# Attention heads in a written TensorE order, a new stacking of q, and the last v projection in a slot of its own

## The chip, the cores and the metric

The kernel runs on one core of a Trainium2 chip. The metric is the device time of one launch in microseconds, as a median of three runs. TensorE multiplies matrices and transposes, into PSUM; VectorE, ScalarE and GpSimd do the elementwise work; SyncE's queue (and for a few small loads ScalarE's) issues the DMA transfers.

## The reference

One layer of a decoder on 512 positions of 1024 columns: a half-step SwiGLU FFN, a mixer with two groups of 8 attention heads of 64 columns, and a second half-step FFN. Each is normed before and after and modulated by a conditioning vector. The change concerns the mixer alone:

```python
p = n @ w_in[l]
qa, ka, va, qi, ki, wi, qb, kb, vb = jnp.split(p, IN_SPLITS, axis=-1)
ki = rmsnorm(ki, g_kidx[l])
oa = rmsnorm(dsa_sparse_attention(qa, ka, va, qi, ki, wi, rel_bias), g_out_a[l])
ob = rmsnorm(stick_breaking_attention(qb, kb, vb), g_out_b[l])
o = jnp.concatenate([oa, ob], axis=-1) @ w_out[l]
```

Group A is sparse: an indexer of 8 heads scores each key, `sum_h w_h * relu(q_h . k)`, the 128 best keys of each query stay, and softmax runs over them with a bias by distance. Group B is stick-breaking attention: the weight of key s is `sigmoid(z_s)` times the product of `1 - sigmoid(z_j)` over the keys j between s and the query.

## The kernel before

Every fp32 matrix product is made of three products of rounded parts (high by high, high by low, low by high). `w_load` brings 128x1024 weights over SyncE's queue into one of three buffers `raw`, rounds them (ScalarE, line 132) and subtracts for the low part (VectorE or GpSimd, line 138); `raw` comes free with the subtraction.

A tile framework traces the program and orders each engine's instructions by its own estimate of when they are ready; each engine then runs its list strictly in that order. A block `manual_schedule` keeps the written order for the engines it names. Here it is used for other stages (ScalarE and VectorE in `down`), not in the mixer. Tiles of one tag share a number of buffers, and a new tile waits until an old one is read.

The mixer (`mixer`, lines 605 to 640) runs so:

- `indexer` (from line 678): `proj_block` projects the index keys and three of the four pairs of index queries into four PSUM banks, first half of the positions, then the second. When a bank is done its end step runs. `end_ki` transposes the keys (line 702), norms them with eight scalings (line 716) and transposes them back doubled (line 719). `end_q` splits a pair of query heads and stacks them by `stack`. Then 8 heads x 3 row blocks of scores (lines 739 to 742) are summed up, head by head, with the projection of the first unit between them.
- `topk` (lines 764 to 778): 16 rounds of `max` and `match_replace` for each of three row blocks (256, 384 and 512 columns), on VectorE: 33 steps each. They are traced at the fifth unit, but may run whenever VectorE is free.
- Eight units of two heads, four of group B, then four of group A. `qkv_steps` gives the projections of the next unit as small steps: the load of k's weights, then 4 steps each for k, q and v, of six matmuls each. `fill` runs a step between the parts of the present unit. In `unit` both heads' score tiles (`attn_b`, lines 896 to 906; `attn_a`, 915 to 923) and transposes (`transposed`, line 888) come first, then for each head the product with v (line 863), three fills, a copy and the output transposes (line 871). The last unit's fills are steps of the output projection (`out_steps`).
- `stack` (line 780) puts the high and the low part of a head on top of each other in one tile by three transfers of 64 partitions. The third writes what the first reads, so it waits for it:

```python
a = self.kq_tile(1)[0]
for dst, src in ((a[0:64], x[0:64]), (a[64:128], y[0:64]), (x[0:64], y[64:128])):
    self.nc.sync.dma_start(out=dst.bitcast(F32), in_=src.bitcast(F32))
```

k is stacked twice (high with high, low with low), q once. Tiles of tag `kq` share 13 buffers.
- At the fifth unit stand the bias rows and windows of group A (`bias_windows`: two matmuls, a store, eight loads on ScalarE's queue) and the norm of group B's output (`o_norm`, lines 564 to 585).
- After the mixer, `mixer_out` norms group A's output and `down` finishes the output projection.

## Time and profile before

| | |
|---|---|
| runs | 1100.77, 1100.91, 1100.93 us; median 1100.91 |
| profiled execution | 1099.78 us; span of its instructions 1098.0 us |
| TensorE matmuls | 1056.6 us busy (96%), x5111 |
| TensorE weight loads | 869.1 us (79%) |
| VectorE / ScalarE / GpSimd | 583.5 (53%) / 405.6 (37%) / 146.0 us (13%) |
| granted clock of TensorE, mean | 0.994 |

Busy shares are averages over stages. The first FFN runs to about 390 us, the norm before the mixer to 420, the indexer to 469, the stick-breaking units to 581, the sparse units to 690, the output projection to 727, and the rest is the second FFN, in which TensorE has nearly no idle time. A matmul's end is modelled in a profile: consecutive matmuls overlap in it. "issue" is time in which an engine waited for nothing that the profile shows. Times in rows are from the start of the span.

### The profile page before, as it was taken

Reading aid. Unit: us, or ns where it says so; the run is one execution under the profiler, and the core shown is the slowest. Engines: PE = TensorE matmul, PEld = TensorE weight load, DVE = VectorE, ACT = ScalarE, POOL = GpSimd, SP = SyncE. Lnnn points to the kernel's source line nnn. Section 1 sums busy time; section 2 is a strip of 40 time slices with the busy share of each in tenths; the row PEclk is TensorE's granted clock in tenths of the full one; section 3 lists DMA queues with packets and bytes.
Section 4 is the critical chain, followed back from the end, with each engine's and each line's share of the span. In section 5 each row is a group of like instructions: output and inputs, shape, how many; then the busy total and the mean of one; then the engine's idle time right before and its main releaser. Section 6 shows DMA issues by size and latency. Waiting matters only on the chain.

```text
span 1098.0 us, 13367 instructions
## 1 busy us (share of the span) xinstructions
PE 1056.6 (96%) x5111; PEld 869.1 (79%) x5111; DVE 583.5 (53%) x988; ACT 405.6 (37%) x711; POOL 146.0 (13%) x103
## 2 busy tenths in 40 slices
PE   3899999999999998999999999999999999999997
PEld 2778888888888888877777878789888888888886
DVE  5979888834223174499995444582333333322313
ACT  3342222222212363455556656472232222221221
POOL 2000000000000522423332413320000000000030
PEclk9899999999999999999999999999999999999999
DMA  9969887732222503533334433303333333222222
GB/s 282 294 210 325 297 283 266 248 96 95 91 89 92 164 20 93 144 96 96 92 97 142 132 101 110 116 21 114 96 96 96 96 96 96 96 96 96 96 77 77
DMA packets 171364, 146.06 MB, mean 133 GB/s; under 512 B 7132, under 2 KB 142460, under 8 KB 171300
## 3 DMA queue, kind: packets, MB, share of 16 engines
q1 hardware_dynamic: 169792, 142.97, 42.4%
q10 hardware_dynamic: 1508, 2.24, 0.6%
q8 instruction: 40, 0.66, 0.2%
q14 instruction: 24, 0.20, 0.1%
HBM read 132.04 MB, written 2.13 MB: 122 GB/s over the span
## 4 chain that ended last, share of the span: by engine, by line
PE 82%; DVE 8%; issue 3%; DMA 3%; POOL 2%; ACT 1%; SPq 1%; DVEq 0%; POOLq 0%; ACTq 0%
PE mm L276 15%; PE mm L277 15%; PE mm L278 15%; PE mm L319 8%; PE mm L320 8%; PE mm L318 8%; PE mm L298 3%; PE mm L468 2%; DVE at L904 1%; DMA ra<-in_w_ada_dram 1%; PE at L793 1%; PE at L794 1%; PE tp L888 1%; DMA kq<-kq 1%; POOL rstd L143 1%
## 5 line engine op out<-in xcount | busy, mean ns | idle before, releaser
L132 ACT ACTIVATE wh<-raw 128x1024 fp32r<-128x1024 f32 x156 | 164.3, 1058 | 432.0 <-PE mm L277 139.4
L276 PE MATMUL mm<-nl,wh 128*128 128x512 f32 x808 | 321.2, 398 | 0.0
L277 PE MATMUL mm<-nh,wh 128*128 128x512 f32 x808 | 316.3, 392 | 0.0
L278 PE MATMUL mm<-nh,wl 128*128 128x512 f32 x808 | 316.1, 391 | 0.0
L138 DVE TENSOR_TENSOR wl<-raw,wh 128x1024 fp32r<-128x1024 f32 (+1 forms) x120 | 147.0, 1227 | 223.7 <-ACT wh L132 223.5
L278 PEld LDWEIGHTS mm<-nh,wl 128*128 128x128 f32 x808 | 151.8, 188 | 31.4
L276 PEld LDWEIGHTS mm<-nl,wh 128*128 128x128 f32 x808 | 152.3, 188 | 28.8 <-ACT wh L132 0.3
L277 PEld LDWEIGHTS mm<-nh,wh 128*128 128x128 f32 x808 | 152.0, 188 | 29.0
L320 PE MATMUL mm<-wh,hT 128*128 128x512 f32 x352 | 138.9, 394 | 0.0
L319 PE MATMUL mm<-wh,hT 128*128 128x512 f32 x352 | 138.8, 394 | 0.0
L318 PE MATMUL mm<-wl,hT 128*128 128x512 f32 x288 | 113.9, 396 | 0.0
L138 POOL TENSOR_TENSOR wh<-raw,wh 128x1024 fp32r<-128x1024 f32 x10 | 25.2, 2534 | 653.7 <-ACT wh L132 653.6
L521 DVE TENSOR_TENSOR sg<-sg,mm 128x512 f32<-128x512 f32 x44 | 30.1, 685 | 105.1 <-PE mm L278 91.0
L138 POOL TENSOR_TENSOR wl<-raw,wh 128x1024 fp32r<-128x1024 f32 x27 | 64.7, 2397 | 106.3 <-ACT wh L132 98.1
L320 PEld LDWEIGHTS mm<-wh,hT 128*128 128x128 f32 x352 | 66.2, 188 | 15.6
L319 PEld LDWEIGHTS mm<-wh,hT 128*128 128x128 f32 x352 | 66.2, 188 | 15.5
L153 DVE SCALAR_TENSOR_TENSOR acc<-ra,sc,acc 128x1024 f32<-128x1024 f32 x49 | 62.7, 1279 | 4.5 <-DMA ra<-in_w_ada_dram 4.0
L318 PEld LDWEIGHTS mm<-wl,hT 128*128 128x128 f32 x288 | 54.1, 188 | 13.1
L468 PE MATMUL mm<-nh,wh 128*128 128x512 f32 x96 | 33.7, 429 | 7.2 <-ACT nh L447 6.9
L132 ACT ACTIVATE hT<-sg 128x512 fp32r<-128x512 f32 x44 | 27.8, 632 | 27.4 <-DVE sg L521 27.4
L138 DVE TENSOR_TENSOR pt<-tp,pt 128x512 fp32r<-128x512 f32 (+1 forms) x48 | 27.2, 594 | 18.8 <-ACT pt L132 18.7
L793 PE MATMUL at<-kq 128*128 128x256 f32 (+2 forms) x88 | 31.3, 357 | 3.4 <-DMA kq<-kq 3.4
(208 smaller groups left out, 1244.9 us busy)
## 6 DMA issues: line engine op xcount, KB each, us to landing
ra<-in_w_ada_dram SPq DMA_DIRECT2D x56, 512.0 KB, 5.6
raw<-in_w_ffn_gate_dram SPq DMA_DIRECT2D x44, 512.0 KB, 4.2
raw<-in_w_ffn_up_dram SPq DMA_DIRECT2D x44, 512.0 KB, 4.3
raw<-in_w_ffn_down_dram SPq DMA_DIRECT2D x44, 512.0 KB, 3.4
raw<-in_w_in_dram SPq DMA_DIRECT2D x28, 512.0 KB, 3.5
kq<-kq SPq DMA_DIRECT2D x84, 128.0 KB, 2.4
ra<-in_w_ada_dram SPq DMA_DIRECT2D x32, 256.0 KB, 5.5
raw<-in_w_out_dram SPq DMA_DIRECT2D x8, 512.0 KB, 3.8
```

The source lines that it names most:

```text
L132: return self.nc.scalar.activation(hi, src, AF.Copy)
L138: return a, (eng or self.nc.vector).tensor_sub(lo, src, hi.bitcast(F32))
L153: nc.vector.scalar_tensor_tensor(acc, raw, sc[:, k:k + 1], acc, op0=ALU.mult, op1=ALU.add)
L276: nc.tensor.matmul(ps[0:m, c], w[0][:, k, :], n[1][:, k, c], start=k == 0, stop=False)
L277: nc.tensor.matmul(ps[0:m, c], w[0][:, k, :], n[0][:, k, c], start=False, stop=False)
L278: return nc.tensor.matmul(ps[0:m, c], w[1][:, k, :], n[0][:, k, c], start=False, stop=k == KD - 1)
L298: mm = self.nc.tensor.matmul(ps[0:m, c], wt[:, k, :], nt[:, k, c], start=j + k == 0, stop=j == 2 and k == KD - 1)
L318: nc.tensor.matmul(ps, lh[:, t], wl, start=n == 0, stop=False)
L319: nc.tensor.matmul(ps, ll[:, t], wh, start=False, stop=False)
L320: nc.tensor.matmul(ps, lh[:, t], wh, start=False, stop=n == len(ks) - 1)
L468: nc.tensor.matmul(banks[j], ws[j][l][:, k, :], n[r][:, k, :], start=k + o == 0, stop=k == KD - 1 and o == 2)
L793: nc.tensor.matmul(ps, q[hd][:, t], kl[hd][:, 0:n], start=True, stop=False)
```

## The change

- `slot` takes the place of `unit`. One slot holds the four score tiles of a new head, one fill after each, and behind each of the first three fills a group of transposes of the head before; then a fill, that head's product with v, a fill, and its output transposes. Sixteen heads make sixteen slots, and a last slot has no new head. All that TensorE gets there stays in the written order.
- v is copied into a tile of its own at the projection's end, and transposed one fill into the next unit (`turn_v`). The load of the next k's weights goes to the first step of v's projection. The last unit's k and q projections, its v projection and the output projection are spread over the last slots with empty steps between them.
- q is split into two tiles of a new tag, and four transfers build its two stacked tiles.
- In the indexer, `proj_block` takes steps ahead of a bank's second half (`mids`), and the second half of `end_ki` goes there; the eight scalings become a product and a copy; the low parts of two index weights are made by VectorE instead of GpSimd; the scores go by row block, and steps of the first top-k are traced among them.
- The bias rows are computed in the first unit, their inputs loaded before the indexer; the windows are still loaded at the fifth unit. `o_norm` of group B becomes four steps ahead of fills of the fifth unit.

The diff, cut to its core:

```diff
-    def proj_block(self, ws, n, banks, ends=()):
+    def proj_block(self, ws, n, banks, ends=(), mids={}):
...
+                if half == 1 and b in mids:
+                    mids[b]()
...
+            for u in range(len(cols) - 1):
+                steps[u][8] = both(first[u + 1], steps[u][8])
+            for k, f in zip((4, 8), loads):
+                steps[-1][k] = both(f, steps[-1][k])
+            gap = [lambda: None]
+            kq, v = steps[-1][:8], steps[-1][8:]
+            steps[-1] = kq[:2] + gap + kq[2:4] + gap + kq[4:] + gap * 2
+            steps.append(v + gap + [outs[0]] + [last[-1]] + [outs[1]] + gap * 2 + [outs[2], outs[3]] + gap + outs[4:])
+            for u in range(len(cols) - 1):
+                steps[u + 1][1] = both(last[u], steps[u + 1][1])
+            self.steps = [first[0]] + steps[0]
...
-            with tc.issue_after(load.ins):
+            with tc.issue_after(load.ins), tc.manual_schedule(engines={mybir.EngineType.PE}):
+                old = None
+                for u in range(len(cols)):
+                    self.steps = steps[u + 1]
+                    if u == 4:
+                        for f in top:
+                            f()
+                        U = self.bias_windows(scr)
...
+                    for hd in range(2):
+                        if u == 4 and hd == 1:
+                            for k, f in enumerate(self.o_norm(1, self.o, oT, tp, pool, 3)):
+                                self.steps[4 + k // 2] = both(f, self.steps[4 + k // 2])
+                            self.o = None
+                        if u == 0 and hd == 1:
+                            scr = self.bias_rows()
...
+                        self.slot(new, old)
+                        old = new
+                self.slot(None, old)
...
-        ws += [(self.w_cols(w_in, C_QI + j * 128, 128, alloc if j == 2 else None,
-                            nc.gpsimd if j < 2 else None), 128) for j in range(3)]
+        ws += [(self.w_cols(w_in, C_QI + j * 128, 128, alloc if j == 2 else None), 128) for j in range(3)]
...
-            for i in range(NT):
-                for c in range(2):
-                    nc.vector.tensor_scalar(k2[:, i, c, :], kk[:, i, :], r[:, i:i + 1], None, op0=ALU.mult)
+            nc.vector.tensor_mul(k2[:, :, 0, :], kk, r.unsqueeze(2).to_broadcast([128, NT, 64]))
+            nc.vector.tensor_copy(k2[:, :, 1, :], k2[:, :, 0, :])
+            st["k2"] = k2
+
+        def end_ki2():
+            k2 = st["k2"]
...
-        self.proj_block(ws, n, banks, [end_ki] + [lambda ps=ps: end_q(ps) for ps in banks[1:]])
+        self.proj_block(ws, n, banks, [end_ki] + [lambda ps=ps: end_q(ps) for ps in banks[1:]],
+                        {3: end_ki2})
...
-        todo = [f for hd in range(6) for f in scores(hd)]
+        todo = [score(*c) for c in [(1, hd) for hd in range(6)] + [(2, hd) for hd in range(3)]
+                + [(1, 6), (1, 7)] + [(2, hd) for hd in range(3, 8)] + [(3, hd) for hd in range(8)]]
...
+        for k, f in enumerate(todo):
+            f()
+            if k % 3 < 2:
+                self.fill()
+            if k > 6:
+                tops[0].pop(0)()
+        return notsel, tops[0] + [f for fs in zip(*tops[1:]) for f in fs], load
...
-            q = self.kq_tile()
+            q = [pool.tile([128, 512], F32R, tag="tm", name="tm", bufs=2) for _ in range(2)]
...
-            st["q"] = self.stack(q[0], q[1])
+            st["q"] = a, b = self.kq_tile()
+            for dst, src in ((a[0:64], q[0][0:64]), (b[64:128], q[0][64:128]), (a[64:128], q[1][0:64]), (b[0:64], q[1][64:128])):
+                nc.sync.dma_start(out=dst.bitcast(F32), in_=src.bitcast(F32))
...
+        def turn_v():
+            vt = st["vt"]
...
+    def slot(self, new, old):
+
+        for i in range(NT):
+            if new:
+                new["tile"][i]()
+            self.fill()
+            if old and i < 3:
+                self.transposed(old, i)
+        if old:
+            self.fill()
+            self.product(old)
+            self.fill()
+            self.output(old)
+        else:
+            self.fill(2)
```

## Rows read from the trace of the kernel before

**Rows 1.** Engine use by stretch: length; busy us of PE, PEld, DVE, ACT, POOL; clock; DMA.

```profile
436.00:466.00 30.00, 30.00 (x143) 25.05 (x143) 13.00 (x22) 14.28 (x29) 12.04 (x8) 1.00 0.56 148
466.00:581.00 115.00, 110.05 (x588) 86.72 (x587) 111.28 (x258) 62.20 (x137) 38.43 (x21) 1.00 0.36 98
581.00:690.00 109.00, 107.62 (x582) 87.20 (x583) 51.58 (x132) 64.19 (x149) 34.54 (x19) 1.00 0.42 122
```

**Rows 2.** Waits of PE, 466 to 690 us: us in total, times, longest.

```profile
PE at L793 <- DMA kq<-kq: 3.4, 4, 1.2
PE tp L888 <- DVE x L906: 2.3, 5, 0.6
```

**Rows 3.** Timeline of PE: start, length, instruction.

```profile
489.66 1.46 PE L863 MATMUL at<-pt,v 128*128 128x512 f32 x8
490.95 0.45 PE L276 MATMUL mm<-nl,wh 128*128 128x512 f32 x1
...
491.70 0.40 PE L276 MATMUL mm<-nl,wh 128*128 128x512 f32 x1
...
492.39 0.39 PE L276 MATMUL mm<-nl,wh 128*128 128x512 f32 x1
```

**Rows 4.** Timeline of PE in the indexer; idle time before in brackets.

```profile
424.87 0.52 PE L298 MATMUL mm<-nh,wh 128*128 128x256 f32 x3
426.35 0.33 PE L719 MATMUL tp<-ident,k 128*128 128x128 f32 x1 [0.97 <-DVE k L716]
...
428.82 0.33 PE L719 MATMUL tp<-ident,k 128*128 128x128 f32 x1 [1.90 <-DVE k L716]
```

**Rows 5.** Engine use by stretch, in the indexer.

```profile
430.00:432.00 2.00, 2.00 (x12) 2.00 (x11) 1.30 (x3) 1.11 (x2) 0.00 (x0) 0.52 0.83 242
432.00:434.00 2.00, 2.00 (x14) 2.00 (x13) 0.58 (x1) 1.09 (x2) 0.00 (x0) 0.62 0.41 96
```

**Rows 6.** Chain that ended last, near 490 us: start, length, what.

```profile
486.33 1.07 ACT wh L132
487.47 2.42 POOL wl L138
489.91 0.37 SPq L120
490.37 3.88 DMA kq<-kq
```

**Rows 7.** Timeline of DVE in the indexer.

```profile
425.88 3.53 DVE L716 TENSOR_SCALAR k<-kk,rstd 128x64 f32<-128x64 f32 x8 [1.13 <-POOL rstd L143]
```

**Rows 8.** Groups on DVE by shape, 469 to 581 us: busy us, mean ns, idle.

```profile
L904 DVE TENSOR_TENSOR_SCAN at<-at,ones 128x512 f32<-128x512 f32 x8 | 9.8, 1222 | 0.2
...
L772 DVE MAX8 m<-tk 128x8 f32<-128x256 f32 x15 | 6.2, 415 | 0.0
L775 DVE MATCH_REPLACE8 tk<-m,tk 128x256 f32<-128x256 f32 x15 | 6.1, 409 | 0.0
...
L906 DVE TENSOR_TENSOR x<-at,x 128x511 f32<-128x511 f32 x8 | 5.4, 676 | 0.0
```

**Rows 9.** Timeline of DVE ahead of the norm before the mixer.

```profile
387.62 0.21 DVE L339 TENSOR_SCALAR ss<-ss 128x1 f32<-128x1 f32 x1 [13.04 <-ACT f L332]
```

**Rows 10.** Tile view of the top-k: ns min/median/max, first and last start.

```profile
L778 DVE TENSOR_TENSOR ns<-tk,sco x3: 680/1640/2115, 572.7 to 576.3; 128x256 bf16<-128x256 f32 x1, 128x384 bf16<-128x384 f32 x1, 128x512 bf16<-128x512 f32 x1
```

**Rows 11.** Groups on ACT by shape, 466 to 581 us: busy us, mean ns, idle.

```profile
L902 ACT ACTIVATE x<-at 128x512 f32<-128x512 f32 x8 | 4.8, 599 | 7.1 <-PE at L900 7.1
```

**Rows 12.** Tile view of the stacked tiles, 466 to 690 us: ns min/median/max.

```profile
L138 POOL TENSOR_TENSOR kq<-q,kq x7: 1282/1301/1471, 489.8 to 659.2; 128x512 fp32r<-128x512 f32 x7
...
DMA to landing us min/median/max: 2.2/2.7/4.4
```

**Rows 13.** Timeline of PE around a group of two transposes and one matmul.

```profile
474.50 0.40 PE L277 MATMUL mm<-nh,wh 128*128 128x512 f32 x1
...
475.26 0.28 PE L793 MATMUL at<-kq 128*128 128x256 f32 x1
```

More of the change, by code (lines that the diff above doesn't have):

```diff
@@ L585, in o_norm @@
             self.normed = self.split(oT[0][:, :, ts], oT[1][:, :, ts], x, nc.vector if i % 2 else nc.gpsimd)
+        return [lambda i=i: one(i) for i in range(NT)]
     def bank(self, pool):
@@ L595, in mixer_out @@
             oT = [[pool.tile([128, 4, S], F32R, tag=f"oT{c}", name="oT", bufs=1) for c in range(2)], oTb]
-            self.o_norm(0, oa, oT[0], tp, pool)
+            for f in self.o_norm(0, oa, oT[0], tp, pool):
+                f()
             g = self.gate_row(1, pool)
@@ L640, in mixer @@
-        return o, banks
+            first, last, steps, ready = map(list, zip(*[self.qkv_steps(*c) for c in cols]))
+            both = lambda *fs: lambda: [f() for f in fs]
+            loads, outs, banks = self.out_steps(oT)
+            for u in range(len(cols) - 1):
[4 more added lines that the diff above has]
+            kq, v = steps[-1][:8], steps[-1][8:]
@@ L642, in out_steps @@
+        return self.o, banks
     def out_steps(self, oT):
-        banks = [self.bank(p) for p in (self.pj, self.pj, self.pj, self.at)]
-        cks = []
+        banks, cks = [], []
         def load(n):
@@ L650, in mms, with run, bias_rows @@
         def mms(i, c):
-            return lambda: self.down_mms(banks[i], lambda k: [t[:, k - 4, :] for t in oT], OUT_KS, i, cks[c])
-        return [load(0), load(2)] + [mms(i, c) for c in range(2) for i in range(NT)], banks
-    def bias_windows(self):
-        nc, pool, pj, d = self.nc, self.pool, self.pj, self.d
-        hot = pool.tile([32, 640], F32, tag="p", name="hot", bufs=3)
-        rb = pool.tile([32, NH], F32, tag="rb", name="rb")
-        nc.scalar.dma_start(out=hot, in_=d["onehot"])
-        nc.scalar.dma_start(out=rb, in_=d["rel_bias"])
-        fr = pool.tile([NH, 640], F32, tag="p", name="fr", bufs=3)
+            def run():
+                if not banks:
+                    banks.extend(self.bank(p) for p in (self.pj, self.pj, self.pj, self.at))
+                self.down_mms(banks[i], lambda k: [t[:, k - 4, :] for t in oT], OUT_KS, i, cks[c])
+            return run
+        return [load(0), load(2)], [mms(i, c) for c in range(2) for i in range(NT)], banks
+    def bias_rows(self):
+        nc, pool, pj = self.nc, self.pool, self.pj
+        rb, hot = self.table
+        fr = pool.tile([NH, 640], F32, tag="pt", name="fr", bufs=4)
         for c0, c1 in ((0, 512), (512, 640)):
@@ L752, in indexer @@
         end_q(ps)
-        for f in todo + scores(6) + scores(7):
-            f()
-            self.fill()
         notsel, tops = [self.tri_gt], []
@@ L835, in end_v @@
             st["v"] = v
-        steps = [weights(ck)]
+        steps = []
         both = lambda *fs: lambda: [f() for f in fs]
@@ L844, in qkv_steps @@
             steps += mms
-        return steps, st
+        return weights(ck), turn_v, steps, st
     def fill(self, n=1):
@@ new lines, in product @@
+    def product(self, h):
+        nc, pool, at = self.nc, self.pool, self.at
+        v, hd = h["v"]["v"], h["hd"]
+        ps = at.tile([128, 512], F32, tag="at", name="at")
+        c = 0
+        for j in range(NT):
+            w = (NT - j) * 128
+            for p in h["pt"]:
+                nc.tensor.matmul(ps[:, j * 128:512], v[:, j, hd, :], p[:, PT_OFF[j]:PT_OFF[j] + w],
+                                 start=c == 0, stop=c == 7)
+                c += 1
+        h["ot"] = pool.tile([128, 512], F32, tag="w2", name="ot", bufs=3)
+        nc.scalar.activation(h["ot"], ps, AF.Copy)
@@ new lines, in transposed @@
+    def transposed(self, h, g):
+        if g == 0:
+            h["pt"] = [self.pool.tile([128, 1280], F32R, tag="pt", name="pt", bufs=4) for _ in range(2)]
+        c0, c1, js = ((0, 512, (0,)), (512, 1024, (1, 3)), (1024, 1280, (2,)))[g]
+        t = self.tp.tile([128, 512], F32, tag="tp", name="tp")
+        for j in js:
+            for i in range(j, NT):
+                c = PT_OFF[j] - c0 + (i - j) * 128
+                s = P_OFF[i] + j * 128
+                self.nc.tensor.transpose(t[:, c:c + 128], h["p"][:, s:s + 128], self.ident)
+        self.split(h["pt"][0][:, c0:c1], h["pt"][1][:, c0:c1], t[:, 0:c1 - c0])
@@ L923, in attn_a @@
             nc.scalar.activation(pp, pp, AF.Exp, scale=-1.0, bias=nm[:, i:i + 1], accum_out=den[:, i, hd:hd + 1])
-            self.fill((0, 1, 1, 2)[i])
-        return p
+        return p, [lambda i=i: one(i) for i in range(NT)]
 @with_exitstack
```

127 lines of the change are left out of this document (49 added, 78 removed).

## The prediction

> **What bounds the kernel now.** Read first how busy the engines are in the mixer, by stretch [rows 1]. From 436 to 466 us (scores of the indexer) TensorE has no idle time. From 466 to 581 us (the four stick-breaking units) it idles 115.00 - 110.05 = 4.95 us, and in the four sparse units, 581 to 690 us, 1.38 us. So TensorE bounds all three, and only its idle time and its clock can be won. The same rows show a second engine close behind: VectorE is busy 111.28 of 115 us in the stick-breaking stretch, because the top-k steps fill it, and only 13.00 of 30 us in the stretch before.
>
> Next, what TensorE waits for between 466 and 690 us [rows 2]: 3.4 us in 4 waits before the first q*k product of a unit (line 793, for the copies that stack q and k), and 2.3 us in 5 waits before the transposes of a head's weights (line 888, for VectorE's last product). With two smaller ones that is the 6.3 us of idle time of rows 1, in 11 waits. The profile makes each too short: a 512-column matmul is drawn 0.40 us long though three starts in steady flow lie 0.69 us apart, 0.23 each [rows 3], so 0.17 us of a wait lies under a drawn end. 6.3 + 11 x 0.17 = 8.2 us.
>
> Third, the indexer. TensorE idles 0.97 and 1.90 us before two of the four transposes of the normalised index keys (line 719) [rows 4]. Right after, its granted clock is 0.52 and then 0.62 of full speed for 2 us each [rows 5], a mixture of the two levels 1.2 and 2.4 GHz; the 5 us before hold the two pauses.
>
> Last, why q arrives late, in the chain of waits at the unit border near 490 us [rows 6]: GpSimd's subtraction of weights frees a buffer, SyncE's queue then issues the weight load that waited for it, and only behind that the copies of q, which take 3.88 us.
>
> **The change, part by part.**
>
> *Index keys.* Eight scalings of 64 columns, 3.53 us from 425.88 [rows 7], become a product and a copy of 256 columns; a pass of VectorE over 256 columns takes 0.41 [rows 8], so 0.8 us, and the keys are ready near 426.7. Their transposes are now traced behind the third bank. When TensorE paused at 425.4, it had done 3 of that bank's 24 matmuls [rows 4]; the other 21 at half of 0.23 us fill 2.4 us, so it comes to the transposes near 427.8, 1.1 us after the keys. Both waits go: 2.87 + 2 x 0.17 = 3.2 us (0 if the keys were late again). The slow clock follows the pauses; without them 2 x 0.48 + 2 x 0.38 = 1.7 us come back (0 if another pause takes their place).
>
> *Two subtractions of weights* move from GpSimd to VectorE, which has 13.04 us without work just there [rows 9]: 0. Without that cover each would hold up the norm by its length, less than GpSimd's 2.42 [rows 6].
>
> *Scores and top-k.* The scores go by row block instead of by head, so the first top-k (256 columns) can start early, 13 of its 33 steps among the scores: 13 x 0.41 [rows 8] = 5.4 us of VectorE's work move into the stretch with 17 us of idle VectorE [rows 1]. 111.3 - 5.4 = 105.9 us are left in the stick-breaking stretch. If that loses its nine waits (4.95 + 9 x 0.17 = 6.5) it lasts 108.5 us, and VectorE is busy 98% of it, as before. On the time: 0. Today the top-k's last result starts at 576.3 us [rows 10], 4.7 us ahead of the first sparse unit; it has 6.5 us less time and 5.4 us less work ahead of it.
>
> *The pipeline.* A slot holds a new head's four score tiles, the former head's three groups of transposes, six fills of six matmuls (1.4 us each), the product with v (1.29 us [rows 3]) and the output transposes (some 0.45). From a head's fourth tile to its first transposes lie four fills, the product, the output and a tile (0.4): 7.7 us. In it ScalarE makes two passes of 0.60 [rows 11] and VectorE one of 1.22 and one of 0.68 [rows 8]: 3.1 us. So the 2.3 us of waits at line 888 and the smaller ones go, unless VectorE's queue holds 4.6 us of other work in front. The written order also takes away TensorE's way out, to put other matmuls ahead of a late operand. Its weak place is the output: between the product and the output transposes stands one fill, 1.4 us, for a copy of 0.60 on ScalarE; behind a rounding of weights of 1.07 [rows 6] it is 0.3 us late. I take 0.1 for each of 16 heads, 1.6 us (0 to 4.8).
>
> *q by four transfers.* Before, three copies, the third held until the first has read; now four from two new tiles without order among them, one issue more per unit on SyncE's queue. From q's last matmul to the next unit now lie four fills, two tiles, two groups of transposes, the product and the output, some 9.1 us. q needs two passes of ScalarE (1.2), 1.30 on GpSimd [rows 12] behind a subtraction of 2.42, and 2.7 (2.2 to 4.4) to land [rows 12]: 7.6, at worst 9.3. All 3.4 us go, or all but 0.2 at a border. The load of the next k's weights is traced four fills earlier, behind q's copies instead of in front: load, rounding and subtraction are the same ones, and only the following copies stand behind it.
>
> *More groups.* The transposes of v stand alone and come one slot step later; the sparse heads have three groups in place of two: some 2 groups more for each of 8 units. A stretch of one matmul, a group of two and one matmul takes 474.50 to 475.26, 0.76 us [rows 13]; two matmuls take 0.46 and two transposes, at half that pitch, 0.23. So 0.07 a group, with 16 of them 1.1 us lost (0 to 1.1).
>
> *Moved off the border.* The bias rows (two matmuls, two copies, a store and, ahead of them, two loads on ScalarE's queue) go into the first unit, the norm of the stick-breaking output into fills of the fifth: the same work, 0. Eight window loads go on ScalarE's queue, six of them into buffers that the top-k frees. Where the queue stands at one of them, ScalarE stands until the top-k ends: 0 to 3 us, taken as 0 since that end lies ahead of the unit. The last output has no fill behind it, but ready matmuls of the second half of the output projection can stand there: 0 to 0.9 (the copy of 0.60 and a share of what is ahead of it), taken as 0.3.
>
> **Sum:** 3.2 + 1.7 + 8.2 - 1.6 - 1.1 - 0.3 = 10.1 us less. The profiled execution took 1099.78 us (span 1098.0, 1.8 around it) and so would take 1089.7; the median of the runs is 1.1 us above it: 1100.9 - 10.1 = 1090.8. What follows the mixer is TensorE with little waiting, so it moves up as a whole. 0.2% (2.2 us) is what a measurement of this kernel can tell from no change.
>
> **The rivals.**
>
> *A, VectorE keeps the stretch.* For it: 97% busy there [rows 1], a fixed order, and top-k steps between the urgent ones. Then the waits for VectorE stay or move to the product: 2.9 us with 7 x 0.17, 4.1 of the 8.2, are not won: 1100.9 - 6.0 = 1094.9 (1093.5 to 1098.7). Against: 4.6 us of slack for each head. The Trainium skill (Perfetto Trace Analysis, Identifying the Most-Contended Engine) judges TensorE by its weight-load share and works first on the engine with the highest occupancy; in this stretch that is VectorE, 97% against 75%, and by that rule this rival is the likely one. The trace has TensorE wait for VectorE's product only 2.3 us.
>
> *B, no change.* The scores by row block hold the eight q tiles of the indexer until the end: with two key tiles and four of the first unit's k 14, and the pool has 13. The last copy of that k waits for a score of the third block; if v's weight load stands behind it in SyncE's queue, the v projection waits for a landing, a rounding and a subtraction, 3.88 + 1.07 + 2.42 = 7.4 us [rows 6], and the slow clock comes again, 1.7: 1100.9 - 1.0 = 1099.9. Against: the load needs nothing from the copy and can be issued first.
>
> *C, slower.* TensorE stands in every slot, since its order can't step aside, for VectorE's last product of the head. It decides at (10.1 + 2.2) / 16 = 0.77 us a slot; at 1 us the time is 1090.8 + 16 = 1106.8. It needs VectorE to answer 5 us late; now it costs TensorE 0.6 us at the longest [rows 2].
>
> *D, slower by the copies.* If q's four half-height copies went one after another, 4 x 2.7 behind 4.9 of preparation is 15.7 against 9.1: 6.6 us at 7 borders, 46 us, near 1141. The Trainium skill (DMA: Bandwidth & Descriptors, Rules for kernel authors) says that transfers to two disjoint halves of the partitions serialise. The rows speak against it at this size: a copy beside a weight load four times its size lands in 3.88 [rows 6], the median is 2.7 [rows 12].
>
> **How the numbers follow.** Forecast (1087 to 1093.5) 0.53; better, down to 1085, if outputs and groups cost nothing, 0.06; A 0.20; B 0.10; C 0.08; D 0.03. Faster is 0.53 + 0.06 + 0.20 = 0.79, the same 0.10, slower 0.11. The range, 1086 to 1100.2, takes in A and B and leaves out C, D and the tip of the better case, some 0.14.
>
> **What would show it.** Right: no pause at the key transposes and full clock to 440 us; no wait of a first q*k product for kq; the former 115 us at 107 to 110, the sparse stretch at 107 to 109. Wrong: transposes or products that wait in most slots, a top-k that ends after the first sparse tile, or a wait between 445 and 470 us for a copy of k or for v's weights.

## The result, and the profile after

The changed kernel takes 1112.72 us (median of 4 runs, 1111.89 to 1113.2) against 1100.92 us of the kernel before: a ratio of 1.0108, 95% interval [1.0096, 1.012]. It is 11.8 us slower where 10.1 us less was forecast. The profiled execution took 1111.89 us, with a span of 1109.6. All times are of fast executions; one execution of `e6_windows_pool`, of 6007.8 us, is left out.

The same stretches as in [rows 1], with the one behind the indexer's pauses and three short ones, in the view of engine use by stretch (length; busy us of PE, PEld, DVE, ACT, POOL; clock; DMA):

```profile
436.00:466.00 30.00, 28.39 (x134) 23.26 (x133) 23.80 (x60) 15.05 (x31) 12.21 (x7) 1.00 0.49 126
466.00:581.00 115.00, 109.05 (x577) 87.22 (x576) 99.16 (x220) 60.92 (x132) 38.76 (x21) 0.99 0.44 120
581.00:690.00 109.00, 100.03 (x527) 81.06 (x534) 50.44 (x121) 60.55 (x137) 29.38 (x16) 0.97 0.32 88
430.00:434.00 4.00, 4.00 (x24) 3.27 (x23) 3.37 (x3) 1.17 (x3) 2.15 (x1) 1.00 0.95 245
493.00:496.00 3.00, 3.00 (x12) 2.52 (x11) 1.63 (x6) 0.94 (x4) 0.00 (x0) 0.50 0.83 224
602.00:605.00 3.00, 3.00 (x10) 2.52 (x11) 2.49 (x6) 1.86 (x4) 0.57 (x1) 0.50 0.65 180
663.00:666.00 3.00, 2.81 (x9) 2.29 (x10) 0.30 (x2) 0.49 (x2) 0.00 (x0) 0.58 0.58 195
```

The part of the indexer that was to be won is won: 430 to 434 us runs at full clock, where [rows 5] had 0.52 and 0.62. But TensorE now idles 1.61, 5.95 and 8.97 us in the three stretches of [rows 1], where it idled 0, 4.95 and 1.38, and its clock is about half in three new places (0.50, 0.50 and 0.58). The waits of PE from 466 to 700 us say what ended the idle time (us in total, times, longest):

```profile
PE tp L931 <- ACT ot L921: 6.2, 3, 4.0
PE at L828 <- issue: 3.1, 1, 3.1
PE tp L202 <- DVE pt L138: 2.5, 1, 2.5
PE at L917 <- ACT pt L132: 1.2, 1, 1.2
PE tp L952 <- DVE oa L935: 1.0, 2, 0.7
PE tp L872 <- DVE ob L935: 0.8, 1, 0.8
PE tp L952 <- DVE pt L138: 0.6, 1, 0.6
PE at L828 <- DMA kq<-tm: 0.6, 2, 0.3
```

The eleven short waits of before ([rows 2] shows nine of them, the longest 1.2 us) have given way to 13, of which five make up 12.3 of 16.0 us. The long ones are not spread over the slots: 4.0 us near 488, 2.5 near 599, 1.5 and 3.1 (with a short one of 0.7) between 646 and 663, and 1.2 in the last slot, near 696. The chain of waits leads back from each of the first three places.

**Near 488 us** (chain that ended last, 482 to 494 us: start, length, what):

```profile
481.14 2.42 POOL wl L138
...
483.57 8.06 DMA raw<-in_w_in_dram
491.63 0.02 issue
491.65 0.33 ACTq L700
...
492.02 0.61 ACT ot L921
...
492.68 1.04 PE tp L931 x4
```

ACTq L700 is a window load of group A, more than 80 us ahead of its use: the framework put the first four on ScalarE's queue as soon as the bias rows were stored. The fourth is issued 0.02 us after a weight load of SyncE's queue has landed. It waits for that transfer's completion, as the framework gave both the same completion counter (in the trace both name semaphore 105), and the head's output copy, ot, stands behind it on ScalarE. The weight load itself takes 8.06 us beside the windows; the median of its kind on the page is 3.7.

**Near 599 us** (timeline of VectorE: start, length, instruction, idle time before in brackets):

```profile
595.28 0.49 DVE L584 TENSOR_SCALAR ob<-ob,rstd 128x512 f32<-128x512 f32 x1 [1.13 <-POOL rstd L143]
...
596.75 1.29 DVE L584 TENSOR_SCALAR ob<-ob,rstd 128x512 f32<-128x512 f32 x1
597.97 0.68 DVE L138 TENSOR_TENSOR pt<-tp,pt 128x512 fp32r<-128x512 f32 x1
598.57 2.95 DVE L584 TENSOR_SCALAR ob<-ob,rstd 128x512 f32<-128x512 f32 x2
601.44 0.41 DVE L138 TENSOR_TENSOR pt<-tp,pt 128x256 fp32r<-128x256 f32 x1
```

The last low part of the head's weights (601.44) reads the buffer that the norm's transposes (line 202) want next. It stands behind the norm's scalings, L584, one of which takes 0.49 us alone and 1.29 or more while GpSimd subtracts (596.47 to 597.75 and 598.87 to 601.23).

**From 646 to 663 us** there is no fill between product and output, since the change put its empty steps there: the transposes come straight behind the product and wait for ScalarE's copy. Then the last unit's first q*k product starts 0.10 us after the third of q's four transfers has landed, at 663.10; the view names no releaser for it (timeline of PE):

```profile
647.49 0.66 PE L931 MATMUL tp<-ident,ot 128*128 128x128 f32 x4 [0.69 <-ACT ot L921]
...
659.47 0.66 PE L931 MATMUL tp<-ident,ot 128*128 128x128 f32 x4 [1.50 <-ACT ot L921]
663.20 0.35 PE L828 MATMUL at<-kq 128*128 128x256 f32 x1 [3.07 <-issue]
```

### The profile page after: what moved, and what is told of

It reads as the page before. It is cut to its first block, busy times and chain, and to the rows that moved or that the text cites. A ratio compares the mean times of both kernels' runs of the same rounds, so it can differ in the third digit from the quotient of the medians.

```text
span 1109.6 us, 13358 instructions
## 1 busy us (share of the span) xinstructions
PE 1060.5 (96%) x5103; PEld 872.3 (79%) x5111; DVE 588.3 (53%) x984; ACT 408.1 (37%) x711; POOL 141.7 (13%) x101
## 4 chain that ended last, share of the span: by engine, by line
PE 44%; DVE 7%; DMA 3%; issue 2%; ACT 1%; POOL 1%; SPq 0%; POOLq 0%; DVEq 0%; ACTq 0%
PE mm L276 8%; PE mm L277 8%; PE mm L278 8%; PE mm L321 4%; PE mm L322 4%; PE mm L320 4%; PE mm L300 3%; DVE tk L810 1%; DVE at L968 1%; DVE m L807 1%; DMA kq<-tm 1%; DVE pt L138 1%; PE tp L952 1%; PE at L828 1%; DMA raw<-in_w_in_dram 1%
## 5 line engine op out<-in xcount | busy, mean ns | idle before, releaser
L138 DVE TENSOR_TENSOR wl<-raw,wh 128x1024 fp32r<-128x1024 f32 (+1 forms) x122 | 149.4, 1227 | 236.8 <-ACT wh L132 236.6
L322 PEld LDWEIGHTS mm<-wh,hT 128*128 128x128 f32 x352 | 66.2, 188 | 15.6
L138 POOL TENSOR_TENSOR wl<-raw,wh 128x1024 fp32r<-128x1024 f32 x25 | 59.9, 2397 | 99.1 <-ACT wh L132 93.4
L828 PE MATMUL at<-kq 128*128 128x256 f32 (+2 forms) x88 | 34.2, 389 | 5.5 <-issue 3.1
L132 ACT ACTIVATE pt<-tp 128x512 fp32r<-128x512 f32 (+1 forms) x48 | 25.2, 524 | 30.0 <-PE tp L952 26.6
```

The source lines that it names most:

```text
L132: return self.nc.scalar.activation(hi, src, AF.Copy)
L138: return a, (eng or self.nc.vector).tensor_sub(lo, src, hi.bitcast(F32))
L322: nc.tensor.matmul(ps, lh[:, t], wh, start=False, stop=n == len(ks) - 1)
L828: nc.tensor.matmul(ps, q[hd][:, t], kl[hd][:, 0:n], start=True, stop=False)
```

## The experiments

Differences are taken from medians. Most of a kernel's own executions lie within 1.7 us of its median; single ones of e5, d4 and e7 lie 2.6, 3.0 and 5.9 us above. Ratios are to the kernel before, run beside each set of kernels, and its medians differ from set to set (1100.92 to 1101.81 us): a difference between kernels of two sets is uncertain by about 0.9 us. Differences taken from the ratios agree with those given here within that.

### Each pause by itself

**e1_windows_spread**: one window load per head's slot.

```diff
-                        U = self.bias_windows(scr)
+                        if u * 2 + hd > 6 and len(U) < NH:
+                            with tc.issue_after(self.mark.ins):
+                                U.append(self.bias_window(scr, len(U)))
```

> The changed kernel with its eight window loads spread out, one per head's slot from the last stick-breaking slot on, each behind that slot's first pass of ScalarE. Theory (pauses add up: a few operands come late at single places, each stops TensorE once and the half clock that follows costs 1.2 to 1.7 us more): the fourth window load stood on ScalarE's queue until a weight load of SyncE's queue had landed, so the pause of 4.0 us before the output transposes near 488 us and the slow clock behind it (1.7) go: 1112.7 - 5.8 = 1106.9 us (1105.5 to 1108.5), no wait of line 931's transposes over 1 us between 470 and 500 us, and the weight load issued near 483.6 lands in under 5 us in place of 8.1. Rival (the pauses cover each other: what TensorE gains in one place it waits for in the next, as q's copies and the top-k are as late as before): at most 2 us less, 1110.7 or more.

Measured: 1125.86 us, ratio 1.0218 [1.0201, 1.0235], 13 us slower still. The pause near 488 is gone, but a far longer one took its place. Timeline of PE:

```profile
574.97 0.40 PE L278 MATMUL mm<-nh,wl 128*128 128x512 f32 x1
595.36 0.90 PE L953 MATMUL tp<-ident,x 128*128 128x128 f32 x3 [20.00 <-DVE pt L138]
```

The top-k's results in the tile view (ns min/median/max, first to last start), here and in the changed kernel:

```profile
L814 DVE TENSOR_TENSOR ns<-tk,sco x3: 395/553/692, 478.9 to 593.8; 128x256 bf16<-128x256 f32 x1, 128x384 bf16<-128x384 f32 x1, 128x512 bf16<-128x512 f32 x1
```

```profile
L813 DVE TENSOR_TENSOR ns<-tk,sco x3: 396/668/1467, 477.6 to 552.6; 128x256 bf16<-128x256 f32 x1, 128x384 bf16<-128x384 f32 x1, 128x512 bf16<-128x512 f32 x1
```

The last top-k ends near 594 us instead of 553. The framework had spread the top-k over the stick-breaking units; here no top-k step ran between 480 and 545 us, and what was left stood in front of a head's low parts. So this run measures two things, and the next one was made to part them.

**e5_windows_late**: the loads traced where they were, held back by an edge alone.

```diff
-                        U = self.bias_windows(scr)
+                        with tc.issue_after(self.mark.ins):
+                            U = self.bias_windows(scr)
```

> The changed kernel with the eight window loads traced where the change has them (so the top-k keeps its place in VectorE's order), but held on ScalarE's queue behind the first pass of the fourth unit's first head, some 65 us later. Theory (pauses add up): the 4.0 us pause near 488 us and the slow clock behind it go and nothing takes their place: 1112.7 - 5.8 = 1106.9 us (1105.5 to 1108.5); the top-k's last result stays near 550 us. Rival 1 (pauses cover each other): a load now stands on ScalarE's queue near 560 to 575 us as long as it did at 488, or VectorE takes the stretch: 1110.7 or more. Rival 2 (what the run with the loads spread out showed, top-k steps put off): a pause of 20 us near 575 again, over 1120; against it, the loads are traced before the fifth unit's work again.

Measured: 1108.74 us (1.0073 [1.0056, 1.009]), 4.0 less than the changed kernel; the top-k ends at 549 again. The theory's mechanism held, with a gain 0.2 us below its range: the wait for ot is gone from 470 to 580 us and 488 to 496 us run at full clock, but q's copies are waited for a little longer. Both e1 and e5 hold the loads back, and e1 alone moves the place where they are traced: so that place is what kept the top-k early. Why (the windows reuse the score buffers) is argued, not shown.

**e6_windows_pool**: the loads on GpSimd's queue (`nc.gpsimd.dma_start` in `bias_windows`).

> The changed kernel with the eight window loads on GpSimd's queue in place of ScalarE's, at the same place of the trace. Theory (the load itself is harmless; what costs is ScalarE's copies standing behind it): the pause near 488 us goes, 1106.9 us (1105.5 to 1109), even if the weight load beside the windows still takes 8 us to land. Rival (the windows' traffic is what costs: the weight load and q's copies that land in 8 us beside it): a wait for q's stacked tiles or for weights of 2 us or more in the same place, 1110 or more.

Measured: 1111.4 us (1.0093 [1.0077, 1.011]), 1.3 less. The rival holds: ScalarE is free, and TensorE stands in the same place for q's copies instead, which land in 4.4 to 4.8 us beside the windows (timeline of PE):

```profile
493.56 0.36 PE L828 MATMUL at<-kq 128*128 128x256 f32 x1 [2.70 <-DMA kq<-tm]
```

So the windows do harm at that time on either queue, through the copies behind them and through the traffic.

**e2_norm_scalar**: the norm's four scalings on ScalarE.

```diff
-            nc.vector.tensor_scalar(o[:, i, :], o[:, i, :], r[:, i:i + 1], None, op0=ALU.mult)
+            nc.scalar.activation(o[:, i, :], o[:, i, :], AF.Copy, scale=r[:, i:i + 1])
```

(for group B alone)

> The changed kernel with the four scalings of the stick-breaking output's norm on ScalarE, not VectorE. Theory (pauses add up): the pause of 2.5 us before the second group of the norm's transposes near 599 us comes from four scalings of 0.49 to 1.5 us in VectorE's queue ahead of the low part of the head's weights; it goes with the slow clock behind it (1.4): 1112.7 - 4.0 = 1108.7 us (1107.5 to 1110.5). Rival (pauses cover each other): ScalarE's four passes of 0.6 us hold the exp of the fourth tile and the wait turns up at the product or the output, 1111.5 or more.

Measured: 1109.59 us (1.0072 [1.0057, 1.0087]), 3.1 less, as the theory had it; no wait at line 202 is left there.

**e3_last_unit**: no empty steps in the last unit's projections.

```diff
-            kq, v = steps[-1][:8], steps[-1][8:]
-            steps[-1] = kq[:2] + gap + kq[2:4] + gap + kq[4:] + gap * 2
-            steps.append(v + gap + [outs[0]] + [last[-1]] + [outs[1]] + gap * 2 + [outs[2], outs[3]] + gap + outs[4:])
+            steps.append(gap + [last[-1]] + gap * 2 + outs[0:2] + gap * 3 + outs[2:5] + gap * 2 + outs[5:6] + gap + outs[6:8])
```

> The changed kernel with the last unit's projections in the twelve fills of the unit before, as for every other unit (no empty steps, v not in a slot of its own), and the eight steps of the output projection spread over the last three slots, two of them always around the product. Theory (pauses add up): the waits of 0.7 and 1.5 us of the output transposes near 647 and 659 us, the 3.1 us of the first q*k product of the last unit near 663 and the slow clock behind it (1.35) go, as no fill stood there: 1112.7 - 7.2 = 1105.5 us (1103.5 to 1108). Rival (the last unit has too little work to cover itself, and v was put there for that): the same waits turn up in the last unit's own slots between 660 and 700 us, 1110 or more.

Measured: 1106.55 us (1.0044 [1.0029, 1.0059]), 6.2 less, as the theory had it. In the last unit only waits of 1.1 us and less are left.

**c1_three**: e5, e2 and e3 together.

> The changed kernel with three edits together: the window loads held to the fourth unit, the norm's scalings on ScalarE (alone 3.1 us less), the last unit's projections in the fills of the unit before (alone 6.2 us less). Theory (pauses add up): 1112.7 - 5.8 - 3.1 - 6.2 = 1097.6 us (1096 to 1099.5), faster than the kernel before. Rival (pauses cover each other: VectorE or the copies become the bound once the large pauses are gone): 1101 or more.

Measured: 1097.12 us (0.996 [0.9945, 0.9975]). The theory held: the three account for 15.6 of the 21.9 us between forecast and result, 2.3 more than their sum of 13.3.

**e7_index_alone**: the kernel before with `mids`, `end_ki2` and VectorE's subtractions of the diff, and nothing else.

> The kernel before with the index keys' part of the change alone: their transposes behind the third bank's second half, a product and a copy for the eight scalings, all low parts of the index weights on VectorE. Theory (this part brought its gain, which the pauses of the pipeline used up): the two waits and the slow clock go, 1100.9 - 4.9 = 1096.0 us (1095 to 1097.5). Rival (what the indexer gains is waited for later, since VectorE is busy 97% of the stick-breaking stretch): 1099 or more.

Measured: 1096.94 us (0.9967 [0.9955, 0.998]), 4.0 less. Its profile is of the slowest of ten executions, 1102.85 us, and shows no wait at the key transposes; the extra time lies ahead of the indexer. This part alone does as much as the whole repaired change; so the repaired pipeline by itself still brought nothing, and the next runs ask why.

### What the repaired pipeline still lost

**d2_old_stack**: `c1_three` with q stacked as before.

```diff
-            q = [pool.tile([128, 512], F32R, tag="tm", name="tm", bufs=2) for _ in range(2)]
+            q = self.kq_tile()
...
-            st["q"] = a, b = self.kq_tile()
-            for dst, src in ((a[0:64], q[0][0:64]), (b[64:128], q[0][64:128]), (a[64:128], q[1][0:64]), (b[0:64], q[1][64:128])):
-                nc.sync.dma_start(out=dst.bitcast(F32), in_=src.bitcast(F32))
+            st["q"] = self.stack(q[0], q[1])
```

> The kernel with the three edits (1097.1 us) with q stacked as before, by three transfers, the third behind the first. Theory (the four transfers shorten the way of q, and the slot has no more slack than that: first q*k products still wait 0.5 us at borders with them): a landing of 2.3 us more less one issue of 0.5 at each of 7 borders, 1097.1 + 7 x 1.8 = 1109.7 us (1104 to 1112). Rival (the slot's cover hides the third transfer too): 1099 or less.

Measured: 1094.39 us (0.9937 [0.9922, 0.9951]), 2.7 less where 12.6 more was expected. Landing of the stacked tiles' transfers, in the tile view of `c1_three` and of this kernel (min/median/max):

```profile
DMA to landing us min/median/max: 2.2/3.5/5.0
```

```profile
DMA to landing us min/median/max: 2.2/2.3/5.3
```

Behind 465 us no q*k product waits for kq here; in `c1_three` three wait 0.3 us each. So the slot's cover hides the three transfers, as the rival had it. The code explains why: of the three transfers only the first two make up the first head's tile; the third completes the second head's, which is wanted a slot later. Of the four, the first head needs the first and the third, and all four share the way.

**f3_pair_order**: `c1_three` with the first head's two transfers issued first.

```diff
-            ((a[0:64], q[0][0:64]), (b[64:128], q[0][64:128]), (a[64:128], q[1][0:64]), (b[0:64], q[1][64:128]))
+            ((a[0:64], q[0][0:64]), (a[64:128], q[1][0:64]), (b[64:128], q[0][64:128]), (b[0:64], q[1][64:128]))
```

> The kernel with the three edits (1097.1 us), q by four transfers, but the two that make up the first head's tile issued first. Theory A (what the three transfers won was that the first head waits for two transfers only): 1097.1 - 2 = 1095.1 us (1094 to 1096), as the low part's transfer goes out one issue earlier. Theory B (it is the four transfers beside each other and beside the weight load that land in 4 us each, where two take 2.3): no change, 1096.5 or more.

Measured: 1095.1 us (0.9942 [0.992, 0.9964]), 2.0 less: theory A, to the number, which is in part luck (the two kernels ran in different sets, and their intervals overlap). Here too no product behind 465 us waits for kq, with four transfers: it was the order of the four.

**f2_old_stack_only**: the same undoing on the changed kernel.

> The changed kernel (1112.7 us) with one part undone: q stacked by three transfers as before. Theory (the four transfers make the first head's tile later, by some 0.4 us at a border that waits and 1.2 us at the first unit): 1112.7 - 2.7 = 1110.0 us (1108.5 to 1111.5). Rival (the forecast's: they save the third transfer's way): slower, 1114 or more.

Measured: 1111.23 us (1.0087 [1.0067, 1.0107]), 1.5 less. The sign is the theory's, the size not quite beyond the runs' scatter. The pause near 488 us is as long as ever: no window load holds up ot here, but the first q*k product waits 4.1 us for q's copies. So the traffic of the windows alone is enough for it, as in e6.

**d1_scores**: `c1_three` with a later place for the fourth pair's first scores.

```diff
-        todo = [score(*c) for c in [(1, hd) for hd in range(6)] + [(2, hd) for hd in range(3)]
-                + [(1, 6), (1, 7)] + [(2, hd) for hd in range(3, 8)] + [(3, hd) for hd in range(8)]]
+        todo = [score(*c) for c in [(1, hd) for hd in range(6)] + [(2, hd) for hd in range(6)]
+                + [(1, 6), (1, 7)] + [(2, hd) for hd in range(6, 8)] + [(3, hd) for hd in range(8)]]
```

(with three fills after four scores, and the top-k steps from the eleventh on)

> The kernel with the three edits (1097.1 us) with the scores of the fourth pair of index heads for the first row block put three scores later, and the first unit's projection steps after three scores of four in place of two of three. Theory (the wait of 1.3 to 1.5 us before a score near 445 us is for the copies of the last pair, which the order by row block asks for three scores too early, and the 1.2 us before the first unit near 464 is for q's copies): both go, 1097.1 - 2.7 = 1094.4 us (1093.5 to 1096). Rival (the first top-k starts three scores later, VectorE ends it later and waits turn up in the stick-breaking units): 1096.5 or more.

Measured: 1095.18 us (0.9942 [0.9926, 0.9959]), 1.9 less. The wait before a score near 445 us is gone.

**d4_by_head**: `c1_three` with the scores head by head, no top-k step among them.

> The kernel with the three edits (1097.1 us) with the scores head by head as before, and no top-k step traced among them. Theory (the order by row block costs the two waits of 2.7 us near 445 and 464 us and buys an early top-k that is not needed, as its last result comes some 20 us ahead of the first sparse unit): 1097.1 - 2.7 = 1094.4 us (1093.5 to 1096). Rival (VectorE, with 5.4 us more work behind 466 us, holds up transposes and the first sparse unit): 1099 or more.

Measured: 1099.66 us (0.9981 [0.9971, 0.9992]), 2.5 more: the rival's time. Its mechanism, VectorE holding up transposes and the first sparse unit, is not what the profile shows: the last top-k result comes at 561 instead of 549 us, and with it the last window loads (near 571) run beside the next unit's q, for which TensorE waits 2.5 us. That profile is of the slowest of ten executions (1102.65 us), so whether the others have this wait is not shown. The order by row block with its early top-k is worth its place by the time; why stays open.

**d3_free_order** and, on the changed kernel, **e4_free_order**: TensorE taken out of `manual_schedule`.

```diff
-            with tc.issue_after(load.ins), tc.manual_schedule(engines={mybir.EngineType.PE}):
+            with tc.issue_after(load.ins):
```

> The changed kernel without the written order on TensorE: the slots are traced as they are, and the framework orders TensorE's instructions by its estimates. Theory (pauses add up at late operands, wherever TensorE's list is made in advance): the operands (ScalarE's copy behind the window load, q's stacked tiles, the norm's scalings) come as late as before, 1109 to 1115 us, with a pause over 3 us near 488 again. Rival (the written order itself is what costs, since TensorE could step aside before): the pauses go and it comes to 1104 or less.

> The kernel with the three edits (1097.1 us) without the written order on TensorE. Theory (without the late operands the written order and the framework's own differ little; what the free order won on the changed kernel was the last unit, 7.8 us against 6.2 for that unit's repair): 1097.1 +- 1.5 us. Rival 1 (the framework's order steps aside where the written one stands): 1094.5 or less. Rival 2 (the written order is what keeps the cover between product and output): 1100 or more.

Measured: 1104.94 us (1.0029 [1.0018, 1.004]), 7.8 less than the changed kernel, and 1094.03 us (0.9932 [0.9917, 0.9947]), 3.1 less than `c1_three`. Both came out lower than the theory had it, the first near its rival's bound, the second inside that of its first rival. The late operands did stay (e4, timeline of PE):

```profile
494.32 0.90 PE L931 MATMUL tp<-ident,ot 128*128 128x128 f32 x3 [3.88 <-ACT ot L921]
```

but in the last unit the framework filled the empty places: from 640 to 690 us TensorE is busy 47.78 us in d3 and 46.31 in `c1_three`.

**f1_all** (d1, d2, d3 together on `c1_three`) and **f4_written** (d1 and d2, written order):

> The kernel with the three edits (1097.1 us), with the later scores (alone 1.9 us less), the three transfers of q (2.7) and the framework's own order on TensorE (3.1). Theory (these are separate lateness in separate places; the later scores and the three transfers share the wait near 464 us, some 1.2): 1097.1 - 1.9 - 2.7 - 3.1 + 1.2 = 1090.6 us (1089.5 to 1092). Rival (they share more, VectorE with the top-k being the one limit behind all of them in the stick-breaking units): 1092.5 or more.

> The same, with TensorE's order written as in the change. Theory (the framework's order wins in the sparse units alone, where it fills the slots of the last unit, 2 us of stretch): 2 to 3 us above the run with all edits, 1092.5 to 1094. Rival (with three transfers nothing is late and the two orders are equal): within 1 us of it.

Measured: 1093.4 us (0.9927 [0.9911, 0.9942]) and 1094.64 us (0.9936 [0.992, 0.9951]). Three repairs worth 7.7 us one by one bring 3.7: the rival, a common limit. `f1_all` is faster than both kernels, by 0.7% than the one before. The intervals of `f1_all` and `f4_written` overlap, so what the written order costs by itself stays open. The chain of waits of `f1_all` near 519 us shows the limit:

```profile
515.78 0.59 DVE x L972
516.37 1.19 DVE tk L812 x2
517.56 1.05 DVE m L809 x2
518.61 0.08 DVE tk L812
518.70 0.38 issue
519.07 0.73 DVE tk L812 x2
519.80 0.34 DVE ob L935
...
520.19 0.67 PE tp L872 x4
```

Between two urgent steps VectorE works through six top-k steps (two `max`, L809, and four `match_replace`, L812) in its fixed order; the addition that frees the buffer for v's transposes (ob, L935) comes 3.4 us after the end of the urgent product (L972) ahead of them. Its operand had been ready since 517.10 us (timeline of ScalarE):

```profile
516.72 0.38 ACT L934 ACTIVATE ob<-tp 128x256 f32<-128x256 f32 x1
```

**g1_half_topk** (`TOPK // 16` for `TOPK // 8` in `topk`) and **g2_v_later** (`turn_v` two fills later):

> The kernel with all edits (1093.4 us) with 8 rounds of the top-k in place of 16 for each row block, which leaves out half of the choosing of keys (32 fewer steps of 0.4, 0.5 and 0.67 us for a block each, some 25 us of VectorE's work). Theory (what is left of the waits in the stick-breaking units, 5.5 us in all behind VectorE's output addition and its low parts of the weights, comes from urgent steps that stand behind top-k steps in VectorE's fixed order): most of it goes, 1093.4 - 4 = 1089.4 us (1088.5 to 1091). Rival (the waits come from the chain of the slot itself, output transposes, ScalarE's copy, addition): 1092.4 or more.

> The kernel with all edits (1093.4 us) with the transposes of v two fills later in the slot. Theory (they wait 1.0 to 1.2 us at three borders of the stick-breaking units since they ask for the buffer that the output addition reads, one fill after the output transposes): 1093.4 - 3.4 = 1090.0 us (1089 to 1091.5). Rival (VectorE is behind by then and the next transposes wait in their place): 1092.4 or more.

Measured: 1088.99 us (0.9889 [0.9874, 0.9905]), 4.4 less, and 1094.87 us (0.9939 [0.9927, 0.9952]), 1.5 more. `g1_half_topk` leaves out half of the choosing of keys: 48 steps, 16 for each row block, not 32 (the 25 us fit 48). Waits of PE from 436 to 700 us in `f1_all`, then `g1_half_topk`, then `g2_v_later`, the lines behind VectorE:

```profile
PE tp L872 <- DVE ob L935: 2.9, 3, 1.1
PE tp L202 <- DVE oa L587: 1.6, 1, 1.6
PE tp L952 <- DVE pt L138: 0.9, 2, 0.7
PE at L917 <- DVE pt L138: 0.5, 1, 0.5
...
```

```profile
PE tp L202 <- DVE oa L587: 1.6, 1, 1.6
PE at L830 <- DVE sco L774: 0.8, 1, 0.8
PE tp L952 <- DVE oa L935: 0.3, 1, 0.3
...
```

```profile
PE tp L872 <- DVE pt L138: 4.6, 3, 1.9
...
```

With half of the top-k steps the waits of the stick-breaking units nearly vanish. With v's transposes moved they wait for another step of VectorE, and longer. It is VectorE's queue, not the place of one step.

An earlier run says the same with the whole top-k. In `e1_windows_spread` its steps stood still from 480 to 545 us. Engine use by stretch in `c1_three`, which has the same pipeline there with the top-k in it, and in two stretches of e1:

```profile
482.00:545.00 63.00, 61.61 (x330) 49.46 (x330) 63.00 (x144) 34.69 (x76) 22.81 (x13) 1.00 0.42 109
```

```profile
482.00:545.00 63.00, 62.58 (x338) 50.89 (x338) 35.96 (x61) 35.83 (x80) 24.55 (x14) 1.00 0.42 109
545.00:570.00 25.00, 25.00 (x138) 20.38 (x136) 25.00 (x58) 14.00 (x30) 8.09 (x5) 1.00 0.52 137
```

Without top-k steps beside it TensorE idles 0.42 us, with them 1.39. Two units, from the first head's product to the fifth's, take 57.1 us in the kernel before (482.19 to 539.28), 54.9 in `c1_three` (487.25 to 542.16), 56.9 in `f1_all` (484.36 to 541.21), but 53.3 in e1 (487.07 to 540.34) and 53.2 in `g1_half_topk` (484.88 to 538.07). So with VectorE out of the way the pipeline does win 3.8 us in two units, where the forecast counted 6.5 in four. From 545 to 570 us VectorE is full in e1 too, and yet TensorE does not idle: a full VectorE alone does not hold it up, what stands ahead of each urgent step does. In e1 the steps put off cost 20 us later; an order of the whole top-k that leaves the urgent steps free was not tried.

## Why the prediction was wrong, point by point

- **Index keys, 4.9 us: right.** Alone they bring 4.0 (the interval of the ratio allows 2.2 to 5.0), and the pauses of [rows 4] and the slow clock of [rows 5] are gone. The two subtractions on VectorE cost nothing that shows.
- **Moved off the border, 0: wrong, and the step that failed first.** The window loads cost 4.0 us (e5) and the norm of the stick-breaking output 3.1 (e2). The prediction named the danger, ScalarE standing behind a window load, but looked for it at the fifth unit and with the top-k's buffers as its cause. It stood 90 us earlier, on the completion of a weight load of another queue; and with ScalarE out of the way (e6, f2) the same place waits for q's copies beside the windows. "The same work" was no price: what counts is which urgent step stands behind it, and which transfers run beside it.
- **The last unit, 0.3 us for its tail: wrong, 6.2 us.** The empty steps were never priced slot by slot. The prediction called the single fill between product and output the weak place; with the steps written out, two slots have none, and behind the last matmuls of q no fill is left to hide its way. In all other slots that fill was enough: in `c1_three` no output waits for ScalarE's copy, so the 1.6 us taken for 16 heads was too much.
- **q by four transfers, "all 3.4 us go": near in size, wrong in cause.** In the repaired kernel 0.9 us of these waits are left (`c1_three`), and with the old three transfers none (d2): the slot's longer cover takes them away, not the four transfers. The step that failed is that the third transfer was taken to be on the way to the first product. It is not; and with four issued in the written order the first head's tile came later. The order costs 2.0 us (f3) in the repaired kernel. The sum of preparation and landing, 7.6 us against 9.1 of cover, left out that the transfers lie behind a weight load in SyncE's queue, which waits for GpSimd.
- **Scores and top-k, 0: a term mis-sized.** Two new waits stand in the changed kernel (0.8 us near 445, 0.7 near 463), the first for copies that the order by row block asks for too early; other places won 1.9 (d1). The order by row block with the early top-k is worth its place, by the time of d4.
- **Head-stage waits on VectorE, 2.3 us: not won.** They went for the most part to the transposes of v. This is **rival A**, hidden in the changed kernel behind the pauses, which gave VectorE time: it is busy 99.16 of 115 us there. Its 1094.9 us is about where the repaired and retuned kernels end (1093.4 to 1095.2); that the numbers meet is in part luck, as these kernels differ from the change in q's order, the scores and the last unit. The rule cited for it from the Trainium skill (Perfetto Trace Analysis, Identifying the Most-Contended Engine), to work first on the engine with the highest occupancy, agrees with g1: 4.4 us for half of the top-k. The last row of e1 above shows its limit, a full VectorE beside a TensorE that does not wait.
- **Rival C** had the sign and a time of 1106.8, but not the mechanism: no pause in every slot, and the order is not what made operands late (e4 has the longest pause too). **B** did not come: no projection waits for v's weights. **D** did not come: in `c1_three` four copies issued from 512.57 to 514.44 us land 4 us after their issue, beside each other (the last of the four left no record of its landing).
- **More groups, 1.1 us:** no run parts this from the rest; it stays open.

Taken together, 21.9 us parted forecast from result: 15.6 for the three pauses with their slow clock, 3.7 for q's order, the scores and the order on TensorE, and 2.6 still there in `f1_all`, for which g1 and e1 point to VectorE's queue. The pipeline does take the late copies off the unit borders, but with the top-k steps in the order that the framework gave them, waits for VectorE take back what it wins.

## What to carry to other kernels

Where a load is moved ahead of its use, price what stands behind its issue on the issuing engine, and ask which transfer's completion it may wait for; here the framework issued it as soon as its data was there. Where an order is written by hand, write each slot out, empty steps too, and look for two dependent steps without work between them. Of several transfers, count those that the first consumer needs, and issue these first. Where an engine mixes urgent steps with steps that can wait, look at what stands ahead of each urgent one, not only at how busy the engine is.

## What was not expected of the hardware

A scaling of 128x512 on VectorE takes 0.48 us in the kernel before, with GpSimd idle, and up to 2.56 us in the changed one, where GpSimd subtracts meanwhile (tile view, ns min/median/max, before, then after):

```profile
L581 DVE TENSOR_SCALAR ob<-ob,rstd x4: 477/482/486, 585.8 to 588.4; 128x512 f32<-128x512 f32 x4
```

```profile
L584 DVE TENSOR_SCALAR ob<-ob,rstd x4: 474/890/2559, 595.3 to 599.0; 128x512 f32<-128x512 f32 x4
```

The Trainium skill (Trainium Architecture — The Big Picture, What this means for kernel authors) says that VectorE and GpSimd share a port pair and that it is an exclusive lock; these rows agree. Both slowed scalings, from 596.75 and 598.96 us, end 0.29 us after GpSimd's subtraction beside them does.

The pauses of 4.0, 2.5 and 3.1 us were each followed by some 3 us at about half clock (0.50, 0.50 and 0.58 above). The clock rows behind the two waits of [rows 4], 0.97 and 1.90 us, had shown the same, and a pause of 1.90 us in `g2_v_later`, before 552.77 us, was followed by 3 us at 0.58. Behind single waits of 1.3 us and less in `c1_three` the mean clock of 436 to 574 us is 1.00.
